# A two-layer hybrid attention kernel: store queues, buffers and loads around its stage borders, and a weave that starts with matrix work alone

## The chip, the cores and the metric

The kernel runs on one core of one Trainium2 chip. The metric is the device time of one execution in microseconds (us), the median of the runs shown. The time before is 3861.09 us, the median of three runs between 3860.72 and 3863.76.

The engines of the core appear under the profile's names: PE is the tensor engine (PEld its weight loads, which run beside the matmuls), DVE the vector engine, ACT the scalar engine, POOL the general-purpose engine and SP the engine that here only issues DMAs. ACT and POOL can issue DMAs too. Each engine takes its instructions in order, DMA issues included.

## The reference

The model has two layers over 2048 latent tokens of width 1024, with 256 context tokens ahead of them, everything in FP32. Cut to what matters:

```
h  = rms_norm(x)  * (1 + scale) + shift          # adaLN; the same for the context, hc
# layer 0 (even): latent attention A and gated linear attention B side by side
q_lat, kv_lat, k_rope, za, gq, gk, gv, g_lr, zb = split(h @ w_in)      # and for hc
q, k, v = mla_heads(q_lat, kv_lat, k_rope)       # 8 heads, 96 wide (64 + 32 rope), values 64
a = softmax(q k^T * scale) v                     # over latent and context keys
b = gla_bidirectional(gq, gk, gv, g_lr)          # scans in both directions, chunks of 64
x = x + gate * (concat(a * silu(za), rms_norm(b) * silu(zb)) @ w_out)  # context too
# layer 1 (odd): neighbourhood attention, 16 heads of 64
q, k, v, z = split(h @ w_in)
o = softmax over an 8 x 16 window of the 32 x 64 grid, with a position bias rpb, and all context keys
x = x + gate * ((o * silu(z)) @ w_out)
```

## The kernel before

The tokens are 18 row tiles (NT) of 128, of which the first two (NCT) are the context; T is all 2304 of them. Every FP32 product of activations with weights is made of three matmuls: each operand is split into a high and a low part (names that end in h or l), and `mm3` adds high x high (L114), high x low (L115) and low x high (L116); `mm3_steps` is the same as a generator, three matmuls to a step (L123 to L125). Attention scores are made of three matmuls in the same way (L889 to L892). Results that a later stage reads in another layout go to DRAM and come back: QT, KT and Vn (queries, keys and values of layer 0, high and low parts), zaT, Un (the other projections of layer 0), Q1, K1, V1, V1c, z1, M1 (those of layer 1), and RT (what the output projection reads).

The softmax has no running maximum. A stage ahead of the attention makes every score once with the high parts alone, reduces it to the maximum of each query row, and stores minus that maximum as one more row of the queries: row A_QK of QT in layer 0, M1 in layer 1. The attention's first matmul (K = 97 or 65 rows) takes it in, so the exponential follows at once.

The stages in order, with their rough place in the profiled span:

- 0 to 573, `even_latent`: for each row tile the first gemm, then `up` (query and key projections, norms, rope) and `fin`: PE transposes into `tp` (L492), the split into `qkhl` (two buffers, ACT and DVE), and four stores to QT and KT from SP (L498). `first(t, j)` makes three of the later projections of the last two tiles ahead, into one buffer `vn`, stored to Un from ACT (L512).
- 573 to 1124, `even_rest`: the remaining projections of layer 0 (`cell`, 86 cells of 8 steps, 688 steps) and the maxima (`maxes`: 8 heads, 83 steps each, 664 in all), matmul L591 and DVE reduction L592, on keys `mk` and queries `mq` loaded from KT and QT (L580, L586). Each head ends with L595 and L597 and the store of its row from ACT (L600).
- 1124 to 2067, `even_mix`: attention (`even_attention`) with the linear attention (`gla`) placed into it. The attention works through 4 pairs of heads, each over 5 query blocks (the context's 256 and four of 512). Keys `akh`, `akl` and queries `aqh`, `aql` have a tile and a load of their own for each head. `gla` loads its rows of Un as `gu` and transposes them (L640, L641).
- 2067 to 2303, `project` of layer 0, with `prep` (norm and transposes L296, L299) of the first two tiles of layer 1 and the first weight loads of it (`od_steps`, buffers `wraw`) running ahead inside.
- 2303 to 2715, `odd_qk`, and 2715 to 3191, `odd_vz`: projections of layer 1. `odd_vz` has 66 cells (528 steps); values go through `ovz` (three buffers) to V1 and V1c (`store_v`), and the maxima of 16 heads (256 steps) are woven in. Each head loads a bias table `mtab`, to which POOL adds masks (L1134, L1135), and stores its maxima to M1 in four pieces.
- 3195 to 3674, `odd_attention`, over 8 pairs of heads: queries q, context keys kc, key blocks kb, values ov, bias tables tab, score matmuls L1244 and L1245. Then `project` of layer 1, to the end.

What sets the order: the Python code emits instructions with their dependences, and a planner that simulates the engines decides the final order on each engine. `weave(main, side, ratio, lag)` steps two generators together, `ratio` steps of the side for one of the main, and bounds how far the main one may be placed ahead: its instructions are issued after the side's step that lies `lag` back. `ahead` holds generators of later weight loads that are stepped in between (`pump`).

## Time and profile before

| | before |
|---|---|
| median of 3 runs | 3861.09 us (3860.72 to 3863.76) |
| the profiled execution | 3867.9 us, its span 3866.1 us |
| PE busy | 3670.2 us, 95% of the span |
| DVE busy | 2347.1 us, 61% |
| ACT busy | 1475.4 us |
| POOL busy | 1269.1 us |
| DMA | 503.09 MB, mean 130 GB/s |

The page's rows give, for each line and engine, what an instruction writes and reads, its shape and number, its busy time and mean ns, and the idle time of its engine just before it with what ended it. A row of the waits gives engine, tile and line that waited, the engine or DMA and the tile that released it, then the total us, the number of waits and the longest. PE's clock (PEclk) is the share of its full rate that it was granted.

### The profile page before, as it was taken

To read this page: it belongs to the slowest core of one execution; us is meant where nothing else is said; L and a number is where in the kernel's file an instruction comes from. 1 tells how busy PE (TensorE), PEld (TensorE's weight loads), DVE (VectorE), ACT (ScalarE), POOL (GpSimd) and SP (SyncE) were. 2 spreads that over 40 slices of the span, in tenths; PEclk is the share of its full clock that TensorE was granted. 3 is DMA by queue.
4 is the path that set the end of the run, shared out by engine and by line. 5 is a ranking of instruction groups with operands and counts; after the bars stand their busy time and mean duration, and the time that the engine had idled before them with its cause. 6 is when DMAs were issued, how large, how long until landed. Compare 5 with 4: busy or idle time off the path is not lost. (4 is left out here: it accounts for less than half of the span.)

```text
span 3866.1 us, 52721 instructions
## 1 busy us (share of the span) xinstructions
PE 3670.2 (95%) x18388; PEld 2767.7 (72%) x18388; DVE 2347.1 (61%) x4699; ACT 1475.4 (38%) x2928; POOL 1269.1 (33%) x1356
## 2 busy tenths in 40 slices
PE   7999979999979999999999999999999997889899
PEld 4999878888866666555556788888788874555577
DVE  4677757888855556586654344444677765667632
ACT  3555541111115555545553123333322225656610
POOL 0334320000004444454543223333222215667622
PEclk8999989999989999999999999999999998999999
DMA  6455553222241232323514544445544468797553
GB/s 236 138 152 148 155 166 90 75 85 77 69 130 59 75 99 75 90 86 111 148 57 136 164 142 126 131 128 154 176 135 132 138 136 207 182 204 183 146 150 114
DMA packets 387175, 503.09 MB, mean 130 GB/s; under 512 B 30691, under 2 KB 265611, under 8 KB 380424
## 3 DMA queue, kind: packets, MB, share of 16 engines
q1 hardware_dynamic: 339174, 447.83, 41.1%
q10 hardware_dynamic: 47576, 51.37, 4.2%
q8 instruction: 146, 2.39, 0.3%
q14 instruction: 119, 0.97, 0.1%
q0 software_dynamic: 160, 0.52, 0.0%
HBM read 329.68 MB, written 169.93 MB: 129 GB/s over the span
## 5 line engine op out<-in xcount | busy, mean ns | idle before, releaser
L106 ACT ACTIVATE apt<-st 128x512 f32<-128x512 f32 (+1 forms) x592 | 346.1, 592 | 340.7 <-PE st L892 306.3
L592 DVE TENSOR_REDUCE mm<-mx 128x1 f32<-128x512 f32 (+1 forms) x656 | 393.2, 628 | 102.8 <-PE mx L591 95.5
L880 DVE TENSOR_TENSOR acc<-acc,apt 128x512 f32<-128x512 f32 x288 | 253.9, 903 | 174.9 <-ACT apt L106 173.4
L865 PE MATMUL av<-apt,av 128*64 128x512 f32 (+1 forms) x1184 | 306.9, 605 | 0.0
L880 POOL TENSOR_TENSOR acc<-acc,apt 128x512 f32<-128x512 f32 x160 | 216.4, 1366 | 238.6 <-ACT apt L106 237.9
L1291 POOL TENSOR_TENSOR oacc<-oacc,opt 128x341 f32<-128x341 f32 (+6 forms) x336 | 237.4, 738 | 116.5 <-ACT opt L106 92.9
L889 PE MATMUL st<-aqh,akh 97*128 97x512 f32 (+1 forms) x592 | 264.0, 446 | 11.1 <-ACT apt L106 5.8
L591 PE MATMUL mx<-mk,mq 96*128 96x512 f32 (+1 forms) x656 | 239.7, 375 | 9.4 <-DMA mq<-QT 8.5
L1162 DVE CUSTOM_DVE_ANT_1 mx<-mx,mtab 128x225 f32<-128x225 f32 (+13 forms) x576 | 180.8, 341 | 103.5 <-PE mx L1156 56.3
L890 PE MATMUL st<-aql,akh 96*128 96x512 f32 (+1 forms) x592 | 236.0, 399 | 1.2 <-DMA aql<-QT 1.2
L892 PE MATMUL st<-aqh,akl 96*128 96x512 f32 (+1 forms) x592 | 234.7, 397 | 0.0
L889 PEld LDWEIGHTS st<-aqh,akh 97*128 97x128 f32 x592 | 112.7, 191 | 137.9 <-issue 76.5
L106 ACT ACTIVATE u<-gm 128x352 f32<-128x352 f32 (+1 forms) x140 | 69.0, 498 | 357.8 <-PE gm L125 283.8
L1351 DVE TENSOR_TENSOR opt<-st,tab 128x64 f32<-128x64 f32 (+10 forms) x576 | 145.1, 313 | 73.1 <-PE st L1245 51.3
L570 POOL DMA_DIRECT2D Un<-u x2 | 1.4, 676 | 565.6 <-DVE u L559 565.6
L998 POOL TENSOR_TENSOR px<-py,px 128x512 f32<-128x512 f32 x68 | 91.2, 1343 | 283.9 <-DVE py L997 277.2
L865 PEld LDWEIGHTS av<-apt,av 128*64 128x64 f32 x1184 | 76.9, 137 | 143.3 <-issue 139.9
L997 DVE TENSOR_TENSOR py<-pj,gate 128x512 f32<-128x512 f32 x68 | 46.9, 690 | 218.0 <-PE pj L116 217.9
L1134 POOL TENSOR_TENSOR mtab<-mtab,maskq 128x1798 f32<-128x1798 f32 x16 | 51.4, 3212 | 325.0 <-DMA mtab<-rpb_q 251.1
L106 ACT ACTIVATE opt<-opt 128x465 f32<-128x465 f32 (+7 forms) x256 | 122.6, 497 | 53.6 <-DVE opt L1351 47.2
L1244 PE MATMUL st<-q,kt 128*128 128x480 f32 (+5 forms) x256 | 101.0, 406 | 39.1 <-ACT opt L106 20.9
L591 PEld LDWEIGHTS mx<-mk,mq 96*128 96x128 f32 x656 | 122.1, 189 | 22.2 <-issue 8.8
(419 smaller groups left out, 10301.7 us busy)
## 6 DMA issues: line engine op xcount, KB each, us to landing
q<-Q SPq DMA_DIRECT2D x48, 512.0 KB
kb<-K SPq DMA_DIRECT2D x192, 128.0 KB
H<-x ACTq DMA_DIRECT2D x36, 512.0 KB
pr<-RT SPq DMA_DIRECT2D x34, 512.0 KB
adaw<-ada_w SPq DMA_DIRECT2D x64, 256.0 KB
x<-H SPq DMA_DIRECT2D x32, 512.0 KB
wraw<-w_od SPq DMA_DIRECT2D x64, 256.0 KB
mtab<-rpb_q SPq DMA_DIRECT2D x16, 899.0 KB
```

The costliest lines, as they stand in the source:

```text
L106: return self.nc.scalar.activation(out, in_, func, **kw)
L591: mm = nc.tensor.matmul(ps[:, :w], q[:A_QK, (t % 6) * P : (t % 6) * P + P], k[:A_QK, k0 : k0 + w], start=True, stop=True)
L592: nc.vector.tensor_reduce(out=m[:, t, n : n + 1], in_=ps[:, :w], axis=AX.X, op=ALU.max)
L865: nc.tensor.matmul(av[i * 64 : i * 64 + 64, :w], V[:, kt, i * 64 : i * 64 + 64], pts[i][:, :w], start=n == 0, stop=n == len(kts) - 1)
L880: eng.tensor_tensor(out=acc[i][e][:, :w], in0=a[:, :w], in1=pts[i][:, :w], op=ALU.add)
L889: nc.tensor.matmul(ps[:, :w], kh[: A_QK + 1, ks], qh[: A_QK + 1, :w], start=True, stop=False)
L890: nc.tensor.matmul(ps[:, :w], kh[:A_QK, ks], ql[:A_QK, :w], start=False, stop=False)
L892: mm = nc.tensor.matmul(ps[:, :w], kl[:A_QK, kq : kq + P], qh[:A_QK, :w], start=False, stop=True)
L1162: nc.vector.tensor_tensor_reduce(out=s, in0=s, in1=tb[:, ri : ri + rn, ci : ci + cn], scale=1.0, scalar=-3e38, op0=ALU.add, op1=ALU.max, a ...
L1244: nc.tensor.matmul(ps, k1, q1, start=True, stop=False)
L1291: eng.tensor_tensor(out=a, in0=a, in1=pts[i][:, a0 - r0 : a1 - r0, :], op=ALU.add)
L1351: nc.vector.tensor_tensor(out=pt[:, d[0], d[1]], in0=ps[:, d[0], d[1]], in1=tabs[i][:, ri : ri + rn, ci : ci + cn], op=ALU.add)
```

## The change

1. **`weave`** gets `head`: so many main steps run before the first side step. After the side has ended, the anchor of the lag moves on with the main steps. `even_rest` weaves with ratio 1.08 and head 40 in place of 1.0, `odd_vz` with 0.57 in place of 0.5.
2. **`even_latent`**: the last two row tiles store Vn, QT and KT from POOL, and the second half of each result takes a buffer of the tag u in place of qkhl. `first` takes a buffer for each of its three j (lth, ltl, vn) and stores Un from POOL.
3. **Weave stores on POOL**: zaT, Un and the maxima's rows in `even_rest`, V1, V1c and M1 in `odd_vz`.
4. **`even_attention`** loads both heads of a pair, and the high and low parts of the queries, with one DMA each into merged tiles. For the first pair keys and values are cut at 3 and 9 key tiles, and the queries of block 1 are loaded behind the first cut. The next pair's keys are loaded at block 2, its values at block 4.
5. **Project and after**: a third `wraw` buffer for layer 1's weights, one more step between the two preps, and in `odd_attention` the first pair's values are loaded after its tables.

```diff
-    def weave(self, main, side, ratio, lag):
-        due, done = 0.0, []
+    def weave(self, main, side, ratio, lag, head=0):
+        due, done, over = -float(head * ratio), [], 0.0
         while True:
             with ExitStack() as es:
-                if len(done) > lag:
-                    es.enter_context(self.tc.issue_after(done[-lag - 1].ins))
+                n = len(done) - lag - 1 + int(over)
+                if n >= 0:
+                    es.enter_context(self.tc.issue_after(done[min(n, len(done) - 1)].ins))
...
                 r = next(side, None)
-                if r is not None:
+                if r is None:
+                    over += 1
+                else:
                     done.append(r)
...
-        sp, bufs, width = stage or (self.prp, 2, cols)
+        sp, bufs, width = stage or (self.prp, self.wbufs, cols)
...
-                nc.sync.dma_start(self.Vn[:, t, :], ...)
+                (nc.gpsimd if t >= NT - 2 else nc.sync).dma_start(self.Vn[:, t, :], ...)
...
-                        hl = self.tl(sp, [P, 4, 2, P], "qkhl", F32R, bufs=2)
+                        if t >= NT - 2 and h2:
+                            hl = self.tl(sp, [P, LAT_COLS], "u", F32R, bufs=2)[:, :1024].rearrange("p (j s t) -> p j s t", j=4, s=2)
+                        else:
+                            hl = self.tl(sp, [P, 4, 2, P], "qkhl", F32R, bufs=2)
...
-                        nc.sync.dma_start(
+                        (nc.gpsimd if t >= NT - 2 else nc.sync).dma_start(
                             dst[h2 * 4 : h2 * 4 + 4, :, :A_QK, t * P : t * P + P].rearrange("h s d t -> d (h s) t"),
...
-                u = self.tl(sp, [P, LAT_CHUNK], "vn", bufs=1)
+                u = self.tl(sp, [P, LAT_CHUNK], ("lth", "ltl", "vn")[j - 2], bufs=1)
                 self.act(u[:], ps[:])
-                nc.scalar.dma_start(self.Un[t, ...], u[:])
+                nc.gpsimd.dma_start(self.Un[t, ...], u[:])
...
-                    nc.scalar.dma_start(self.zaT[...], z[:])
+                    nc.gpsimd.dma_start(self.zaT[...], z[:])
                 elif j == 1:
-                    (nc.gpsimd if t < 2 else nc.sync).dma_start(self.Un[t, :, 1056:], u[:])
+                    nc.gpsimd.dma_start(self.Un[t, :, 1056:], u[:])
                 else:
-                    nc.scalar.dma_start(self.Un[t, :, (j - 2) * 352 : (j - 1) * 352], u[:, :352])
+                    nc.gpsimd.dma_start(self.Un[t, :, (j - 2) * 352 : (j - 1) * 352], u[:, :352])
...
-                    nc.scalar.dma_start(self.QT[h, 0, A_QK]..., r[:NT].bitcast(F32))
+                    nc.gpsimd.dma_start(self.QT[h, 0, A_QK]..., r[:NT].bitcast(F32))
...
-            self.weave(gemms, maxes(), 1.0, 30)
+            self.weave(gemms, maxes(), 1.08, 30, 40)
...
-            kh = self.tl(ap, [P, T], f"akh{i}", F32R, bufs=2)
-            cuts = (0, half, T) if j == 0 else (0, T)
+            kh = self.tl(ap, [P, 2, T], "akh", F32R, bufs=2)
+            cuts = firsts + (T,) if j == 0 else (0, T)      # firsts = (0, 3 * P, half)
...
+            q = self.tl(ap, [P, 4, 512], "aq", F32R, bufs=2)
+            nc.sync.dma_start(q[:A_QK, :, :w].bitcast(F32), self.QT[2 * j : 2 * j + 2, :, :A_QK, q0 : q0 + w]...)
...
+                early[0], _ = queries(0, 0, CTX)
+                gens = [keys(0), low(0, 0), values(0)]
+                K, L0, V = [next(g) for g in gens]
+                early[1], _ = queries(0, CTX, 512)
+                for g in gens:
+                    next(g)
+                next(gens[0])
+                L = [L0, next(low(0, 1))]
+                next(gens[2])
...
-                if j < 3 and nb > 1:
+                if j < 3 and nb in (2, 4):
                     with self.tc.issue_after(last.ins):
-                        if nb < 4:
-                            nextK[nb - 2], = keys(j + 1, nb - 2)
+                        if nb == 2:
+                            nextK, = keys(j + 1)
...
-            self.prep_pool(e1, "prp1", "left", 2)
+            self.prep_pool(e1, "prp1", "left", 2, 3)
...
                 for t in range(2):
                     hT[t] = self.prep(1, t, self.x1, pp, ("pj", 4))
+                    yield
                     yield
...
-            self.nc.scalar.dma_start(self.V1c[:, t, c], v[:])
+            self.nc.gpsimd.dma_start(self.V1c[:, t, c], v[:])
...
-            self.nc.scalar.dma_start(self.V1[a + r, g * 64 : g * 64 + 64, c], v[r * 64 : r * 64 + 64])
+            self.nc.gpsimd.dma_start(self.V1[a + r, g * 64 : g * 64 + 64, c], v[r * 64 : r * 64 + 64])
...
-                        nc.scalar.dma_start(self.M1[h, ...], ...)
+                        nc.gpsimd.dma_start(self.M1[h, ...], ...)
...
-            self.weave(gemms, maxes(), 0.5, 15)
+            self.weave(gemms, maxes(), 0.57, 15)
...
                 kc = keys(j, 0, CTX, "kc")
-                V = values(j)
...
+                else:
+                    V = values(j)
...
                 tabs = [table(2 * j + i, i) for i in range(2)]
+                if j == 0:
+                    V = values(j)
```

More of the change, by code (lines that the diff above doesn't have):

```diff
@@ L278, in ada_row, with prep_pool @@
             nc.sync.dma_start(self.gates[l, :, (b - 4) * 512 : (b - 4) * 512 + 512], row[:])
-    def prep_pool(self, es, name, side, bufs):
+    def prep_pool(self, es, name, side, bufs, wbufs):
         self.prp = self.pool(es, name, bufs=2, side=side, reuse_waits="tile")
-        self.hbufs = bufs
+        self.hbufs, self.wbufs = bufs, wbufs
     def prep(self, l, t, src, pp, tag):
@@ L808, in low @@
         def low(j, p):
-            kl = [self.tl(ap, [P, half], f"akl{p}{i}", F32R, bufs=1) for i in range(2)]
-            for i in range(2):
-                nc.sync.dma_start(kl[i][:A_QK].bitcast(F32), self.KT[2 * j + i, 1, :A_QK, p * half : (p + 1) * half])
-            return kl
-        def queries(j, q0, w):
-            Q = []
-            for i, h in enumerate((2 * j, 2 * j + 1)):
-                qh = self.tl(ap, [P, 512], f"aqh{i}", F32R, bufs=2)
-                ql = self.tl(ap, [P, 512], f"aql{i}", F32R, bufs=2)
-                nc.sync.dma_start(qh[:A_QK, :w].bitcast(F32), self.QT[h, 0, :A_QK, q0 : q0 + w])
-                nc.sync.dma_start(qh[A_QK : A_QK + 1, :w].bitcast(F32), self.QT[h, 0, A_QK : A_QK + 1, q0 : q0 + w])
-                last = nc.sync.dma_start(ql[:A_QK, :w].bitcast(F32), self.QT[h, 1, :A_QK, q0 : q0 + w])
-                Q.append((qh, ql))
-            return Q, last
@@ L826, in even_attention @@
+        nextK = nextV = None
+        early = {}
         for j in range(4):
-            rest = []
             if j == 0:
-                Q, _ = queries(0, 0, CTX)
-                gens = [keys(0, i) for i in range(2)] + [values(0)]
-                K = [next(g) for g in gens[:2]]
-                L = [low(0, 0)]
-                V = next(gens[2])
-                rest = gens
-            else:
-                K = list(nextK)
-                V = nextV
-                L = [low(j, 0), low(j, 1)]
+                early[0], _ = queries(0, 0, CTX)
[7 more added lines that the diff above has]
+                next(gens[2])
+            else:
+                K, V = nextK, nextV
+                L = [next(low(j, p)) for p in range(2)]
@@ L839, in even_attention @@
             for nb, (q0, w, kts) in enumerate(blocks):
-                if j or nb:
+                if j == 0 and nb in early:
+                    Q = early.pop(nb)
+                else:
                     Q, last = queries(j, q0, w)
@@ L850, in even_attention @@
                 yield
-                if rest:
-                    for g in rest[:2]:
-                        next(g)
-                    L.append(low(0, 1))
-                    next(rest[2])
-                    rest = []
                 av = self.tl(pp, [P, 512], "av", bufs=2)
@@ L1256, in odd_attention @@
                         pass
+                else:
+                    V = values(j)
                 if mk is None:
```

48 lines of the change are left out of this document (27 added, 21 removed).

## The prediction, made before the changed kernel was run

> **What bounds the kernel now.** I read the page's first part, then the waits of the tensor engine over the whole run, then windows cut around the largest of them, then the timelines of the DMA queues there. The page first.
>
> ```profile
> span 3866.1 us, 52721 instructions
> PE 3670.2 (95%) x18388; PEld 2767.7 (72%) x18388; DVE 2347.1 (61%) x4699; ACT 1475.4 (38%) x2928; POOL 1269.1 (33%) x1356
> L592 DVE TENSOR_REDUCE mm<-mx 128x1 f32<-128x512 f32 (+1 forms) x656 | 393.2, 628 | 102.8 <-PE mx L591 95.5
> ```
>
> PE is busy 95% of the span. The change adds and removes no matrix work, so all it can win is PE's idle time, 3866.1 - 3670.2 = 196 us, and what the idle stretches cost in clock afterwards. Where the idle time sits is in the waits: engine, line and what it waited for, then us in total, times, longest.
>
> ```profile
> engine line waited for: us in total, times, longest us
> PE st L1244 <- DMA q<-Q: 12.5, 2, 8.1
> PE gl L641 <- POOL gu L640: 10.3, 1, 10.3
> PE mx L591 <- DMA mq<-QT: 8.5, 1, 8.5
> PE gm L123 <- ACT onat L106: 7.0, 1, 7.0
> PE gm L114 <- ACT vn L106: 6.4, 1, 6.4
> PE tp L438 <- DVE qkhl L496: 5.6, 4, 3.9
> PE st L889 <- DMA aqh<-QT: 5.2, 1, 5.2
> PE pj L299 <- DVE x L296: 4.9, 1, 4.9
> PE mx L597 <- DVE mc L595: 4.4, 2, 2.5
> PE mx L1149 <- ACT mz L106: 3.7, 1, 3.7
> PE tp L492 <- DVE qkhl L496: 3.0, 3, 1.2
> PE mx L1169 <- DVE mc L1167: 2.7, 1, 2.7
> PE st L890 <- DMA aql<-QT: 1.2, 1, 1.2
> PE st L1245 <- DMA kc<-K: 1.2, 1, 1.2
> ```
>
> These are single events at borders between stages, and the windows around them show two costs: PE's busy time short of the window's length, and a granted clock (PEclk) well under 1 for the work that is done there. The columns are PE, PEld, DVE, ACT and POOL busy, PEclk, DMA share, GB/s.
>
> ```profile
> 545.00:558.00 13.00, 6.45 (x24) 6.20 (x25) 8.80 (x18) 4.58 (x7) 4.88 (x4) 0.61 0.91 272
> 573.00:586.00 13.00, 4.47 (x15) 3.93 (x15) 4.19 (x7) 1.01 (x3) 0.00 (x0) 0.61 0.97 244
> ...
> 1121.00:1132.00 11.00, 7.25 (x27) 4.94 (x27) 3.95 (x10) 2.39 (x7) 0.44 (x3) 0.53 1.08 273
> 1132.00:1156.00 24.00, 8.18 (x19) 5.55 (x20) 2.18 (x5) 3.55 (x7) 1.48 (x4) 0.57 0.72 199
> 2183.00:2194.00 11.00, 6.13 (x22) 4.90 (x21) 5.81 (x7) 5.00 (x11) 1.98 (x3) 0.69 0.47 153
> 2714.00:2726.00 12.00, 5.03 (x15) 3.67 (x14) 4.38 (x8) 4.65 (x8) 0.00 (x0) 0.72 0.80 231
> 3182.00:3222.00 40.00, 18.29 (x50) 9.92 (x49) 15.86 (x49) 8.53 (x17) 9.11 (x4) 0.57 1.00 212
> ...
> 600.00:1050.00 450.00, 449.70 (x2330) 398.25 (x2329) 366.25 (x610) 60.37 (x106) 0.00 (x0) 1.00 0.26 78
> ```
>
> So inside the weave (600 to 1050) PE never stops and runs at full clock; at the borders it loses both. I price the clock as busy time in the window times one minus PEclk, since work done at PEclk c would have taken c of that time. The last row also gives a measure for cover: 450 / 2330 = 0.19 us for one matmul of the weave.
>
> **Border 1, latent into even_rest (545 to 586).** The change gives the three Un chunks of `first` a tile each, so the 6.4 us wait on the one vn buffer has no cause left. The last two tiles' result stores go out on POOL, half of their results lie in other buffers, and the weave runs 40 gemm steps before its first max. In the changed program's order 48 matmuls of W2/WU gemms then stand between the last transposes and the first mx, and further gemms split the last kn transposes. What they must hide:
>
> ```profile
> 570.01 1.47 SPq L498 DMA_DIRECT2D KT<-qkhl  x2
> 573.38 0.32 SPq L580 DMA_DIRECT2D mk<-KT  x1
> ```
>
> The load of mk follows the issue of the last KT store, which ends at 570.01 + 1.47 = 571.48, by 1.9 us, and PE waited 8.5 us for mk and mq. 48 x 0.19 = 9.1 us of gemms hide that. The added cost is POOL: its only stores before are these two.
>
> ```profile
> L570 POOL DMA_DIRECT2D Un<-u x2: 556/676/797, 1112.6 to 1120.5; - x2
> ...
> DMA to landing us min/median/max: 2.6/5.3/7.9
> ```
>
> A landing after 2.6 to 7.9 us in place of those 1.9 makes mk later by 0.7 to 6.0; I take 2 of exposure. Ten stores of 0.7 us occupy a POOL that the rows at 573 and 600 show idle. Sum: idle 6.4 + 8.5 + 1.0 (one of the L492 waits) = 15.9; clock (6.45 + 4.47) x 0.39 = 4.3; less 2: **18 us**, bounds 10 and 20. The 3.9 us wait of L438 at 525 stays. If the 48 gemms were not ready (they need W2's weights, loaded long before), the 8.5 us would come back whole.
>
> [...]
>
> **Border 2, even_rest into even_mix (1121 to 1156).** SP and ACT show why the queries came late.
>
> ```profile
> 1124.93 0.30 ACTq L600 DMA_DIRECT2D QT<-mr  x1
> ...
> 1131.56 0.30 SPq L819 DMA_DIRECT2D aqh<-QT  x1
> 1136.69 1.24 SPq L636 DMA_DIRECT2D gu<-Un x2
> ```
>
> The last row of maxes is stored at 1124.93, the next query load is issued 6.6 us later, and the gla's gu load another 5.1 us behind it in SP's order; L889, L890 and L641 pay 5.2 + 1.2 + 10.3. With ratio 1.08 the last max ends before the last gemms (688 gemm steps and 664 max steps; 40 + 664 / 1.08 = 655), the loads are merged (SP has 1368 instead of 1490 instructions over the run), the first key pieces are cut to three key tiles, and block 1's queries go out ahead of the remaining keys. In the changed order the attention's first loads wait only for gemms some 70 to 200 matmuls ahead of its first score, and the first gl transpose stands 71 matmuls = 13.5 us behind it, while gu is issued near the start. Idle 0.7 (a wait of the last mx) + 2.5 + 5.2 + 10.3 + 1.2 = 19.9; clock 7.25 x 0.47 + 8.18 x 0.43 = 6.9; together 26.8. The DMA share of 1.08 and 0.72 says that bytes, not only order, hold the loads; I leave 4 us of wait and 2 of clock: **21 us**, bounds 10 and 27. The stores of zaT, Un and the mr rows on POOL (18 + 68 + some 8 for each max stage) meet a POOL that was busy 0.00 in the weave; ACT loses their issues, where it was busy 60 of 450 us. Both are off the path: nothing.
>
> Faster maxes load DVE: 366.25 / 450 = 81% rises by 1.08 to 88%. That is mostly the reduce of 628 ns for each mx. PE waited on it 0.7 us in all; for the denser weave, and the odd one, I charge 1 us in 100 over the 450: **-5**, bounds 0 and -12.
>
> **The smaller borders.** An extra `yield` between the two preps puts 48 matmuls (9.1 us) ahead of the second one's transposes; the 4.9 us wait for x goes, and 6.13 x 0.31 = 1.9 of clock: **6**, bounds 0 and 7. At 2714 PE waits 7.0 us for onat from ACT, which stands in order behind copies of weights that wait for loads into two wraw buffers; the third buffer lets the loads start one earlier. 7.0 + 5.03 x 0.28 = 8.4 at most; whether one buffer is enough the trace cannot show: **5**, bounds 0 and 8. The gla scan's waits keep their order: nothing, 5 either way.
>
> **Border 3, odd_vz into odd_attention (3182 to 3222).** Idle 40 - 18.29 = 21.7, clock 18.29 x 0.43 = 7.9. With 0.57 the 256 max steps are done after 449 of 528 gemm steps, and five whole cells of 24 matmuls, 120 x 0.19 = 23 us, follow without maxes; the waits for mz and mc (3.7 + 2.7) have work beside them. About 6.4 MB (by the code's shapes: queries, tables, V, the context's keys, the first key block) must land before scores run freely; at the row's 212 GB/s that is 30 us, so 7 stay open, with their clock, and the smaller waits (kc 1.2, and those on opt) stay. V1c's load still waits for the last V1c store, now POOL's. I take **13**, bounds 0 and 24.
>
> **Sum.** 18 + 21 - 5 + 6 + 5 + 13 = 58. The profiled execution took 1.8 us more than its span (3867.9), 6.8 us above the median; single waits are alike in any execution, so I take the sum from the median: 3861.1 - 58 = **3803 us**. All upper bounds together, with the scan's: 20 + 27 + 7 + 8 + 24 + 5 = 91, 3770; all lower ones: 10 + 10 - 12 - 5 = 3, 3858.
>
> **Rivals.** *The loads take it back.* The borders move at 199 to 273 GB/s with a DMA share near 1; if bytes hold them, an earlier issue gains only what the weave's tail lends. Then 2 keeps its gl part, 1 its vn part, 3 nothing: 10 + 12 - 5 + 6 + 0 = 23, 3838. For it: the DMA columns; against: the share is 0.26 in the weave before, where the new loads now begin.
>
> *Slower: POOL's order in odd_vz.* Now some 64 V1 and V1c stores and 64 M1 stores stand in one in-order queue with the adds on mtab.
>
> ```profile
> POOL mtab L1134 <- DMA mtab<-rpb_q: 251.1, 13, 30.8
> L1134 POOL TENSOR_TENSOR mtab<-mtab,maskq 128x1798 f32<-128x1798 f32 x16 | 51.4, 3212 | 325.0 <-DMA mtab<-rpb_q 251.1
> ```
>
> POOL sat 251.1 us at such adds, waiting for the table, 30.8 us at most and 19 on average. A V1 store queued behind such an add is held as long; ovz has three buffers, and at four or more cells of 24 x 0.19 = 4.6 us that is some 14 us of slack, so a 19 us wait costs PE 5 and a 30.8 us wait 17. It decides the sign when the 13 waits cost 5 or more each: 65 - 58 = 7 over. With 2 us of clock behind each gap it is 13 x 7 = 91, and 91 - 58 = 33: 3894. Against it: the planner knows the order and puts stores that are ready ahead of the adds.
>
> *No change.* The order by the changed program does what the diff says, so this needs new waits that sum to 50 to 66; for it speaks only that DVE is next in the weaves.
>
> [...]
>
> **How the numbers follow.** This kernel's measurement can tell 0.2%, 7.7 us, from no change. Forecast 0.68 (its own range 3775 to 3830); loads take it back 0.15; no change 0.04; POOL's order 0.13. Faster: 0.68 + 0.15 = 0.83, same 0.04, slower 0.13. Leaving out the slower case and a few in a hundred at the low end, the range is 3778 to 3850.
>
> **What would show it.** In the changed profile: no wait of gm on vn; mx on mq under 3 us; gl on gu and st on aq under 4 together; pj on x gone; gm on onat under 3; the first q wait near 7; PEclk near 1 around 550, 1140 and 2190; PE idle near 145 us. POOL's waits in odd_vz with ovz copies waiting on DMA would show the slower rival. DVE as PE's releaser by more than 12 us in the weaves, or a POOL store from which an mk load waits over 10 us, would make the forecast wrong.

## The result, and the profile after

The changed kernel takes 3834.48 us (median of four runs, 3830.0 to 3836.73) against 3860.9 us for the one before in the same comparison: a ratio of 0.9924, 95% interval 0.9911 to 0.9937. It is faster by 26 us where 58 were forecast, inside the stated range. The profiled execution took 3835.3 us, its span 3833.5. The profiled span of before was 3866.1, so the two traces differ by 32.6 us and not by 26.4: the profiled execution of before lay 6.8 us above its median, as the prediction noted, and the changed one 0.8. The account below is of the traces.

The page and the waits of PE after, in the same form as before:

```profile
span 3833.5 us, 52744 instructions
PE 3668.1 (96%) x18388; PEld 2758.2 (72%) x18388; DVE 2349.6 (61%) x4699; ACT 1474.7 (38%) x2928; POOL 1413.8 (37%) x1594
...
q0 software_dynamic: 13088, 32.52, 2.8%
```

```profile
PE st L1246 <- DMA q<-Q: 12.8, 1, 12.8
PE mx L604 <- DVE mc L602: 7.2, 7, 1.8
PE gm L123 <- ACT onat L106: 6.0, 1, 6.0
PE tp L442 <- DVE qkhl L503: 4.8, 4, 3.2
PE mx L1171 <- DVE mc L1169: 4.4, 9, 1.0
PE tp L496 <- POOL kn L484: 4.3, 1, 4.3
PE gm L114 <- ACT lth L106: 2.5, 1, 2.5
PE tp L572 <- DVE u L566: 2.0, 1, 2.0
```

Gone are the waits for mq (8.5), vn (6.4), the queries aqh and aql (5.2 + 1.2), gu (10.3), x in `pj` (4.9) and mz (3.7). New are kn behind POOL (4.3), lth (2.5) and u (2.0), and the waits for mc come at 7 of the 8 heads of maxima in `even_rest` and at 9 of the 16 in `odd_vz`. The windows, columns as before:

```profile
520.00:590.00 70.00, 56.48 (x279) 50.03 (x277) 34.48 (x59) 26.91 (x44) 22.86 (x27) 0.88 0.63 188
...
1115.00:1160.00 45.00, 42.45 (x185) 25.64 (x184) 16.79 (x25) 24.18 (x44) 16.30 (x18) 1.00 0.69 187
...
2155.00:2185.00 30.00, 30.00 (x138) 24.81 (x137) 13.04 (x17) 6.66 (x15) 7.16 (x7) 1.00 0.63 212
...
3155.00:3200.00 45.00, 30.41 (x135) 19.25 (x135) 13.85 (x39) 15.53 (x32) 17.70 (x14) 0.81 0.91 223
600.00:1050.00 450.00, 442.92 (x2292) 392.83 (x2291) 367.98 (x619) 58.81 (x103) 43.47 (x75) 1.00 0.24 75
```

The border into even_mix is nearly full and at full clock. But the weave, where PE was busy 449.70 of 450 us before, now has 442.92.

To see where time goes when stages shift, I laid the two traces beside each other at equal amounts of PE work: each matmul counts with the median distance to the next start among its kind, the sums of both kernels are equal, and at each point of the sum the times are subtracted. The table holds what each stretch gained (minus) or lost against before, in us; the first row is the forecast in the same cut, the others are this kernel and the experiments told below. The stretches in before's time: start to 521, border 1 to 627, even weave to 1107, border 2 to 1187, attention and gla to 2060, project 0 to 2270, odd_qk to 2673, the stage change at 2714 to 2760, odd weave to 3161, border 3 to 3307, the rest of PE's work, and the end behind it. Each row is one execution, up to 7 us off its kernel's median. Stretches that a kernel shares with the changed one agree within about 4, project 0 within 5 and the rest of PE's work within 7; border 2 and the attention run into each other, and the cut between them is uncertain by 2. The two kernels told last have no row.

```
                        start  b1  weave    b2  attn  proj   qk  2714  oddw    b3  rest  end
forecast                  0   -18     5   -21    0    -6     0    -5     0   -13     0    0
changed kernel          0.1  -8.9   6.9 -25.0  5.5  -5.6   0.8  -3.4   7.6 -16.0  -0.2  5.5
weave stores back       1.9 -11.4   5.3 -11.8  3.2  -5.3   0.3   0.3   6.4  -6.4   3.5  0.3
even_rest stores back   0.3  -8.1   5.3 -12.0  3.1  -5.5   0.7  -0.2   8.8 -14.9  -0.0  2.3
ratios back             2.3  -8.6  -1.8  -3.9 -1.1  -2.6   1.0  -2.9  -0.5   0.0   5.4  5.4
old attention loads     3.6  -9.0   6.9  -2.4  2.5  -7.1  -0.9  -0.5   9.1 -17.5  -0.7  5.4
merged loads alone      1.2  -0.1   1.6 -15.0 -2.4   0.2  -0.2  -0.1   0.4   0.6  -3.8  0.2
latent stores back      2.3  -8.5   6.9 -25.5  4.4  -3.9   0.4  -2.7   9.6 -15.4  -3.4  0.4
small parts back       -1.4  -5.6   5.3 -23.2  3.4  -0.4  -0.2   4.5   8.6 -13.3   1.7  5.4
V1c load on POOL        1.7 -11.2   5.3 -24.3  6.8  -7.1   0.8  -0.4   9.3 -10.6  -7.2  5.6
late transpose          1.0  -9.7  -3.2 -24.6  4.1  -4.3   0.8  -2.7   2.7 -16.9   1.0  5.4
first pair first        1.8  -8.1  -3.2 -24.8  3.4  -1.1   0.4  -3.1   4.8  -6.8   3.3  5.5
```

So the borders gave 8.9 + 25.0 + 5.6 + 3.4 + 16.0 = 58.9 us, close to the 63 forecast for them, and 25.5 were lost elsewhere: 14.5 in the two weaves where 5 were charged, 5.5 in the attention, 5.5 behind the last matmul.

### The profile page after: what moved, and what is told of

The parts are those of the page before. It is cut to its first block, busy times and chain, and to the rows that moved or that the text cites. A ratio compares the mean times of both kernels' runs of the same rounds, so it can differ in the third digit from the quotient of the medians.

```text
span 3833.5 us, 52744 instructions
## 1 busy us (share of the span) xinstructions
PE 3668.1 (96%) x18388; PEld 2758.2 (72%) x18388; DVE 2349.6 (61%) x4699; ACT 1474.7 (38%) x2928; POOL 1413.8 (37%) x1594
## 3 DMA queue, kind: packets, MB, share of 16 engines
q0 software_dynamic: 13088, 32.52, 2.8%
## 5 line engine op out<-in xcount | busy, mean ns | idle before, releaser
L1296 POOL TENSOR_TENSOR oacc<-oacc,opt 128x341 f32<-128x341 f32 (+7 forms) x336 | 239.1, 742 | 109.3 <-ACT opt L106 81.5
L890 PE MATMUL st<-aq,akh 97*128 97x512 f32 (+1 forms) x592 | 263.1, 445 | 4.0 <-ACT apt L106 3.9
L891 PE MATMUL st<-aq,akh 96*128 96x512 f32 (+1 forms) x592 | 234.7, 397 | 0.0
L893 PE MATMUL st<-aq,akl 96*128 96x512 f32 (+1 forms) x592 | 233.9, 396 | 0.0
L890 PEld LDWEIGHTS st<-aq,akh 97*128 97x128 f32 x592 | 111.9, 189 | 136.5 <-issue 90.7
L893 PEld LDWEIGHTS st<-aq,akl 96*128 96x128 f32 x592 | 113.1, 191 | 31.0 <-issue 5.7
L106 ACT ACTIVATE prh<-pr 128x1024 fp32r<-128x1024 f32 x34 | 35.7, 1056 | 252.1 <-PE pj L115 252.1
L598 PEld LDWEIGHTS mx<-mk,mq 96*128 96x128 f32 x656 | 120.8, 188 | 11.6
```

The lines of the kernel that those rows point to most:

```text
L106: return self.nc.scalar.activation(out, in_, func, **kw)
L598: mm = nc.tensor.matmul(ps[:, :w], q[:A_QK, (t % 6) * P : (t % 6) * P + P], k[:A_QK, k0 : k0 + w], start=True, stop=True)
L890: nc.tensor.matmul(ps[:, :w], K[: A_QK + 1, i, ks], qh[: A_QK + 1, :w], start=True, stop=False)
L891: nc.tensor.matmul(ps[:, :w], K[:A_QK, i, ks], ql[:A_QK, :w], start=False, stop=False)
L893: mm = nc.tensor.matmul(ps[:, :w], kl[:A_QK, i, kq : kq + P], qh[:A_QK, :w], start=False, stop=True)
L1296: eng.tensor_tensor(out=a, in0=a, in1=pts[i][:, a0 - r0 : a1 - r0, :], op=ALU.add)
```

## The experiments

Twelve kernels ran, each timed beside the kernel before.

| kernel | median us | before beside it | ratio, 95% interval |
|---|---|---|---|
| weave stores back | 3847.77 | 3864.92 | 0.9956 (0.9940 to 0.9971) |
| ratios back | 3856.52 | 3864.92 | 0.9973 (0.9962 to 0.9984) |
| old attention loads | 3861.85 | 3864.92 | 0.9992 (0.9982 to 1.0001) |
| latent stores back | 3835.28 | 3864.92 | 0.9925 (0.9909 to 0.9940) |
| small parts back | 3854.62 | 3862.94 | 0.9978 (0.9968 to 0.9988) |
| merged loads alone | 3851.24 | 3862.94 | 0.9963 (0.9948 to 0.9978) |
| late transpose | 3823.43 | 3862.94 | 0.9897 (0.9880 to 0.9914) |
| V1c load on POOL | 3840.39 | 3862.94 | 0.9936 (0.9922 to 0.9951) |
| first pair first | 3838.09 | 3868.51 | 0.9928 (0.9913 to 0.9942) |
| first pair, latent stores back | 3825.14 | 3868.51 | 0.9897 (0.9882 to 0.9911) |
| first pair, kn on DVE | 3831.68 | 3868.51 | 0.9907 (0.9889 to 0.9924) |
| even_rest stores back | 3848.05 | 3868.51 | 0.9954 (0.9939 to 0.9969) |

The kernel before ran slower beside these runs than in the first comparison, so the ratios are compared and not the medians; the expected times were written against 3861. The changed kernel itself was not timed again beside them: its 0.9924 is from the first comparison.

### Weave stores back

```diff
-                    nc.gpsimd.dma_start(self.zaT[...], z[:])
+                    nc.scalar.dma_start(self.zaT[...], z[:])
...
-                    nc.gpsimd.dma_start(self.Un[t, :, (j - 2) * 352 : ...], u[:, :352])
+                    nc.scalar.dma_start(self.Un[t, :, (j - 2) * 352 : ...], u[:, :352])
...
-                    nc.gpsimd.dma_start(self.QT[h, 0, A_QK]...)
+                    nc.scalar.dma_start(self.QT[h, 0, A_QK]...)
...
-            self.nc.gpsimd.dma_start(self.V1c[:, t, c], v[:])          # V1 and M1 in the same way
+            self.nc.scalar.dma_start(self.V1c[:, t, c], v[:])
```

> The changed kernel with the weaves' stores (zaT, Un and the maxima's rows in even_rest; V1, V1c and M1 in odd_vz) back on ACT and SP; the latent stores stay on POOL. In the changed kernel POOL's DRAIN at the very end lasts 9.48 us (1.55 before) and holds the end of the program by some 5.5 us. Theory A (the queue of the weave stores does not matter inside the weaves; the drain grows with the number of DMAs that POOL has issued): the last DRAIN falls to about 2 us, the waits of the maxima's transposes on mc stay (7.2 and 4.4 us), 3829. Theory B (POOL's stores are what freed ACT and SP at the borders): the waits at the borders return, 5 to 15 us in sum, 3840 to 3850. Theory C (POOL's stores hold back DVE in the weaves, and that is why mc is late): the mc waits fall to 4.4 and 3 as before, 3820.

Theory B held: 0.32% of the time, some 12 us, is lost against the changed kernel; by the table 13 us at border 2 and 10 at border 3, less 5 at the end, but this trace lies 6.5 us above its median. C fell: the waits for mc stay. A was right on the last DRAIN alone, 2.71 us here. At border 2 the wait of PE and the queues of ACT and SP behind it read as follows:

```profile
PE st L890 <- ACT apt L106: 13.2, 2, 11.9
```

```profile
1121.91 7.21 SPq L851 DMA_DIRECT2D azt<-zaT  x1
1129.22 0.26 SPq L620 DMA_DIRECT2D ge<-gate_w  x1
```

```profile
1129.70 1.29 ACT L106 ACTIVATE apt<-st 128x512 f32<-128x512 f32 x2 [2.17 <-PE st L893]
1145.24 0.63 ACT L106 ACTIVATE gw<-ge 97x512 fp32r<-97x512 f32 x1 [14.25 <-DMA ge<-gate_w]
1145.78 1.55 ACT L106 ACTIVATE apt<-st 128x512 f32<-128x512 f32 x3
```

PE waits for an st buffer that ACT's exponential frees; ACT stands 14.25 us at the copy of gla's gate weights, because that load went out at 1129.22, behind a load of zaT that held SP for 7.21 us. In the changed kernel the same loads and the same copy are these:

```profile
1118.88 0.34 SPq L851 DMA_DIRECT2D azt<-zaT  x1
1119.33 0.26 SPq L620 DMA_DIRECT2D ge<-gate_w  x1
```

```profile
1135.30 0.63 ACT L106 ACTIVATE gw<-ge 97x512 fp32r<-97x512 f32 x1 [2.01 <-DMA ge<-gate_w]
```

In both kernels the copy starts 16 us after the load was issued; with the stores back the load was issued 10 us later, and PE waited for it through ACT. So the stores act at the border, through the order of SP and then of ACT. Why the load of zaT held SP for 7.21 us, the trace does not say.

### even_rest stores back

Only the stores of even_rest were put back, in the same way.

> The changed kernel with only even_rest's stores (zaT, Un, the maxima's rows) back on ACT and SP; odd_vz's and the latent ones stay on POOL. With all weave stores back the border into even_mix lost 13 us and that into odd_attention some 10 against the changed kernel. Theory A (each border depends on its own stage's stores): the first of the two comes back, the second border stays as in the changed kernel, 3846. Theory B (the stores of odd_vz made all of it): 3835. The last DRAIN, with 154 DMAs from POOL: by their number it would last some 7 us, by the latent stores alone 9.

Theory A: border 2 falls to 12.0, border 3 keeps 14.9. PE's wait for apt is there again, 11.8 us at its longest. Each border depends on its own stage's stores. The last DRAIN took 6.30 us, with 148 DMAs from POOL and not the 154 expected.

### Ratios back

```diff
-            self.weave(gemms, maxes(), 1.08, 30, 40)
+            self.weave(gemms, maxes(), 1.0, 30, 40)
...
-            self.weave(gemms, maxes(), 0.57, 15)
+            self.weave(gemms, maxes(), 0.5, 15)
```

> The changed kernel with the ratios 1.0 (head 40 kept) and 0.5 in the two weaves. Theory A (the denser weave is what makes PE wait for mc, 5.4 us more in even_rest and 6.5 in odd_vz): the weaves win some 9 + 8 us, but the maxima end with or behind the gemms and the borders into even_mix and odd_attention lose 10 to 25 us: 3828 to 3845, and the mc waits in the weaves under 1 us each. Theory B (the borders' gain comes from the order of the loads, not from the weave ending early): borders stay as they are, 3818. Theory C (POOL's stores make the mc waits): the waits stay and the borders lose, 3850.

Theory A, more strongly than expected. The weaves win back 8.7 and 8.1 us, and the borders lose 21 and 16: border 3's whole gain, and all but 4 us of border 2. B and C fell. The end of even_rest shows what an uncovered tail of maxima is:

```profile
1080.00:1100.00 20.00, 20.00 (x94) 16.42 (x93) 14.96 (x25) 2.40 (x4) 2.08 (x3) 1.00 0.64 152
1100.00:1120.00 20.00, 18.74 (x44) 10.23 (x43) 19.40 (x37) 1.88 (x2) 0.56 (x1) 0.67 1.00 261
1120.00:1140.00 20.00, 17.67 (x46) 9.45 (x46) 9.31 (x18) 4.17 (x10) 1.61 (x6) 0.50 0.44 120
```

```profile
1106.40 19.14 PE L598 MATMUL mx<-mk,mq 96*128 96x512 f32 x35 [0.21 <-DVE mm L599]
```

Between 1100 and 1120 DVE is busy 19.40 of 20 us and PE starts 44 matmuls, against 94 in the 20 us before, though its busy column still says 18.74; the clock is at 0.67, then 0.50. The 35 matmuls of maxima from 1106.40 on stand 0.55 us apart, where matmuls of the weave stood 0.21 us apart (20 / 94); DVE's 37 instructions in its 19.40 us keep the same pace. This kernel keeps head 40 at ratio 1.0, so its maxima end later than those of the kernel before: the run shows the price of a late end, and not only the loss of an early one.

### Old attention loads, and merged loads alone

The first puts `even_attention`'s loads of before into the changed kernel, the second puts the new ones into the kernel before; the whole of part 4 of the change, one way and the other.

> The changed kernel with even_attention's loads as before (a tile and a load for each head, cuts at 9 key tiles only, queries of block 1 not ahead). The border into even_mix won 28.6 us against the 21 forecast. Theory A (merged, cut and early loads carry about half of it): waits of the first scores on queries of 5 to 10 us come back with half clock behind them, 3848. Theory B (the maxima that end before the last gemms carry it; loads then start early in either form): border as in the changed kernel, 3835. In both, the 7 us that the attention lost between 1160 and 1340 against before would go if they come from the merged tiles: 3841 or 3828 then.

> The kernel before with only even_attention's new loads (merged tiles, cuts at 3 and 9 key tiles, block 1's queries early); ratios, stores and buffers as before. With the old loads in the changed kernel nearly all of its gain at the border into even_mix went. Theory A (the border is a chain of three links, maxima that end early, their stores on a queue that is free, few early loads, and each alone gains little): within 5 us of before, 3857 to 3865. Theory B (the loads alone carry the border): 15 to 25 us faster, 3840 to 3850.

The first fell on the side of A and beyond it: border 2 keeps 2.4 of 25.0 us, and with the weaves' cost nothing is left of the whole change (0.9992). The waits that return are other ones than I expected, gla's and not the scores':

```profile
PE gl L648 <- POOL gu L647: 9.2, 1, 9.2
PE gl L654 <- DVE gw L624: 6.4, 1, 6.4
```

The second lies between its theories: the loads alone win 15.0 us at border 2, 0.37% in all. So the loads carry more than half of that border by themselves, while ending early and storing from POOL carry almost nothing without them (2.4). With the loads the two add 10. The attention's 5.5 us loss is 2.5 with the old loads, 4.1 with late transposes, and turns to a gain of 1 to 2 wherever the ratios are the old ones. So the merged tiles alone are not its cause; with the uncertainty of the cut, more is not shown.

### Latent stores back

```diff
-                (nc.gpsimd if t >= NT - 2 else nc.sync).dma_start(self.Vn[:, t, :], ...)   # QT, KT too
+                nc.sync.dma_start(self.Vn[:, t, :], ...)
...
-                nc.gpsimd.dma_start(self.Un[t, ...], u[:])
+                nc.scalar.dma_start(self.Un[t, ...], u[:])
```

> The changed kernel with the last two latent tiles' stores of Vn, QT and KT back on SP and those of the first rest chunks back on ACT; the extra buffers stay. In the changed kernel PE waits 4.3 us for kn, whose multiplication stands on POOL behind a store that waits for DVE. Theory A (POOL's in-order stores are that wait): it goes, but SP is blocked in four weight loads for 8.9 us around 545, so the stores go out late and the first mx waits 3 to 8 us on mq: 3832 to 3840. Theory B (SP is not late, 48 gemms hide all): 3829. Theory C (the kn wait comes from DVE's chain, not from POOL's order): the wait stays at 3 to 4 us and mq is added: 3842.

Theory B came nearest: 0.9925 against 0.9924, and border 1 at 8.5 against 8.9. The wait for kn goes and longer waits for qkhl, u and lth take its place. The stores on POOL are worth nothing at border 1; by exclusion the buffers and the 40 steps made its gain, and no run parts these two. The end is shorter by 5 us in this trace (DRAIN 4.25), which the ratios, with intervals of 6 us to each side, do not show. In the changed kernel POOL's queue shows how the kn wait came about:

```profile
557.45 0.82 POOL L505 DMA_DIRECT2D QT<-qkhl  x1 [2.48 <-DVE qkhl L503]
558.26 0.59 POOL L519 DMA_DIRECT2D Un<-ltl  x1
558.85 0.81 POOL L505 DMA_DIRECT2D QT<-u  x1
559.67 0.63 POOL L484 TENSOR_TENSOR kn<-kbase,sqk 128x256 f32<-128x256 f32 x1
```

DVE's part of kn, and PE's transposes behind both:

```profile
557.73 0.68 DVE L483 TENSOR_TENSOR kn<-kn,sqk 128x512 f32<-128x512 f32 x1
```

```profile
560.35 1.94 PE L496 MATMUL tp<-ident,kn 128*96 128x128 f32 x8 [4.27 <-POOL kn L484]
```

The next tile's multiplication stands behind a store that waits for DVE's qkhl of this one, and PE's transposes stand behind the multiplication. But DVE's own part of kn stands behind the same qkhl and was done only at 558.41; POOL's was done at 560.30. So POOL's order makes at most 1.9 of the 4.3 us.

### Small parts back

```diff
-            self.prep_pool(e1, "prp1", "left", 2, 3)
+            self.prep_pool(e1, "prp1", "left", 2, 2)
...
                     hT[t] = self.prep(1, t, self.x1, pp, ("pj", 4))
                     yield
-                    yield
```

and the first pair's values ahead of its tables.

> The changed kernel without its fifth part: two wraw buffers, one step between the two preps, the first pair's values loaded ahead of its tables. Theory A (the account of the changed kernel's trace): the wait of pj on x of 4.9 us and its half clock come back (7 us), the third wraw buffer brought nothing (onat 6.0 against 7.0 before, so within 2), the order of values and tables moves the first q wait by under 3: 3843. Theory B (the prep's cover comes from other moves): 3835, no wait on x.

It cost 0.54%, some 20 us, where theory A said 8. The wait for x came back as expected (5.2 us; project 0 loses 5.2). The third `wraw` buffer was worth far more than the nothing of theory A: 7.9 us at the stage change against the changed kernel. The other kernels with three buffers lie between -3.4 and 0.3 there, so its worth is 4 to 8. Three edits went back at once; that this stretch is the buffer's is argued from its place. The buffer hardly shortens the wait for onat (7.7 here, 6.0 to 7.8 with three buffers), but those of ACT for weights, over the run:

```profile
ACT w3h L106 <- DMA wraw<-w_od: 23.2, 13, 3.5
ACT w1h L106 <- DMA wraw<-w_od: 22.3, 13, 5.0
ACT w2h L106 <- DMA wraw<-w_od: 15.3, 10, 2.7
```

In the changed kernel the same three are:

```profile
ACT w1h L106 <- DMA wraw<-w_od: 14.2, 8, 6.0
ACT w3h L106 <- DMA wraw<-w_od: 10.1, 12, 1.9
ACT w2h L106 <- DMA wraw<-w_od: 8.1, 7, 1.9
```

With two buffers two PE waits of 2.6 us (tp on ovz) and 2.3 us (mx on mm) follow right behind the wait for onat; that the late copies on ACT push this work back is argued. The remaining us are spread over borders 1, 2 and 3 and the rest, none of them over 3.3.

### Late transpose

```diff
-                    ps = self.tl(pp, [P, 512], "mx", bufs=5)
-                    mm = nc.tensor.transpose(ps[:NT, :P], mc[:], self.ident[:])
-                    ...                                  # mr, its store, yield
+                    late = h, mc                         # made behind step 6 of the next head
...
+                            if late is not None and n0 == 6:
+                                mm = close(*late)
+                                late = None
+                                yield mm
```

In odd_vz the same behind the step of R == 3.

> The changed kernel with the transpose of each head's maxima (and the store of its row) moved behind the sixth max step of the next head in even_rest and the fourth in odd_vz. Theory A (PE's loss in the denser weaves is its wait for DVE's reduction of mc, 7.2 + 4.4 us in the groups, some 16 us over both weaves): waits on mc under 2 us in sum, both weaves back near the rate of before, 3822. Theory B (DVE is full at the new ratio, and PE will wait for a free mx buffer instead): waits of mx on mm appear, 3832.

Theory A. All waits on mc are gone from the list, which had 7.2 and 4.4 us of them, and the same window of the weave is full again, at the denser ratio:

```profile
600.00:1050.00 450.00, 450.00 (x2347) 400.18 (x2346) 375.15 (x633) 61.10 (x108) 45.22 (x78) 1.00 0.25 77
```

DVE is busy 375.15 of 450 us, and PE waited for mm only 0.3 us over the whole run, in the odd weave. So DVE was not full at ratio 1.08; PE stood behind a transpose that came in its order before DVE had reduced the last maxima of its head. The ratio, 0.9897, is better than the changed kernel's 0.9924; the intervals (0.9880 to 0.9914 and 0.9911 to 0.9937) just overlap. The odd weave keeps 2.7 us of its loss.

### V1c load on POOL, and first pair first

```diff
-                nc.sync.dma_start(V[:, :NCT, :], self.V1c[:, :, c])
+                (nc.sync if j > 1 else nc.gpsimd).dma_start(V[:, :NCT, :], self.V1c[:, :, c])
```

> The changed kernel with the loads of the context's values of the first two pairs in odd_attention issued from POOL, where their stores are, in place of SP. In the changed kernel SP stands still from 3151 to 3161.4 in front of the load ov<-V1c, and the queries behind it come 12.8 us late for PE. Theory A (that wait in SP's order is the 12.8): the first q wait falls to 4 to 7 us, 3827. Theory B (the loads of kc and q wait for the last gemm's buffers and for bandwidth anyway): the wait stays at 10 or more, 3834.

Theory B's sign came: the first q wait is 15.9 us. The wait for the V1c store that held SP for 10.4 us in the changed kernel (first row) was not, alone, what PE waited for. With it gone, the five loads of V behind it hold SP for 9.10 us (second row), and kc goes out at 3164.64, where it was 3163.93:

```profile
SPq L1234 <- DMA V1c<-ovz: 10.4, 1, 10.4
```

```profile
3154.60 9.10 SPq L1236 DMA_DIRECT2D ov<-V  x5
```

Next the second pair's loads, which SP issues ahead of the first pair's kc and q:

```diff
+                if j == 1:
+                    with self.tc.issue_after(q0last.ins):      # first pair's last query load
+                        V = values(j)
+                        tabs = [table(2 * j + i, i) for i in range(2)]
```

on top of the late transposes.

> The kernel with the late transposes, and in odd_attention the second pair's values and tables held back until the first pair's queries are issued. With the context's values moved off SP the first q wait stayed (15.9 us), so that store was not its cause. Theory A (the second pair's loads, 2 x 517 KB of tables and 8 x 128 KB of values, stand ahead of the first pair's kc and q on SP, and these are issued only at 3164 to 3170, when the last gemms are over): the first q wait falls from 11.9 to 3 to 6 us, with some clock 8 us less, 3815. Theory B (DMA bandwidth holds the border, not the order): the wait falls by under 3, 3822. Theory C (the second pair then starts late, 60 us on): 5 us or more come back there, 3820.

Theory C won: the wait fell by 3, from 11.9 to 9.0 us, and border 3 as a whole lost 10 (6.8 against 16.9). The waits for opt are longer now, by theory C because the second pair starts late:

```profile
PE st L1266 <- DVE opt L1383: 22.5, 22, 6.9
PE st L1266 <- DMA q<-Q: 9.0, 1, 9.0
```

With the late transposes alone the first of them was this:

```profile
PE st L1265 <- DVE opt L1375: 17.6, 25, 1.8
```

The planner's order was better than mine. That the bytes of both pairs set the pace here is not shown; the DMA share of 0.91 between 3155 and 3200 in the changed kernel speaks for it.

### First pair with latent stores back, and with kn on DVE

Both stand on the kernel of "first pair first"; the first adds the edit of "latent stores back", the second that of "V1c load on POOL" and `kn` of the last two tiles on DVE.

> As the run beside it (late transposes, first pair first), and the last two latent tiles' stores on SP, those of the first rest chunks on ACT. Theory A (the POOL stores of the latent border win 2 to 3 us there and cost 5.2 at the end, where POOL's DRAIN lasts 9.48 us with them and 4.25 without): 3812, 3 us under the run beside it. Theory B (the length of the DRAIN goes by something else): DRAIN stays near 9 us and the time is 2 us over the run beside it.

> As the first of these runs (late transposes, first pair first), with the kn multiplication of the last two latent tiles on DVE in place of POOL, and the context's values of the first two pairs loaded from POOL. Theory A (PE's 4.3 us wait for kn comes from POOL's in-order stores, and SP's wait at the load of V1c is next once the second pair is out of the way): the kn wait goes, the first q wait falls by 2 to 4 us against the first run, 3809. Theory B (the kn wait is DVE's chain; q waits for its buffers): both stay within 1 us, 3815.

The first gained against "first pair first" (0.9897 against 0.9928), with the DRAIN at 4.25 us as theory A said, but by 13 us where it said 3. Of the 9.8 us between the traces 5.1 are the end, and 5.5 lie in project 0, which the edit does not touch. The second gained less surely (0.9907, its interval overlaps). There theory A holds for q and not for kn:

```profile
PE tp L496 <- DVE kn L484: 2.8, 1, 2.8
...
PE st L1267 <- DMA q<-Q: 2.7, 1, 2.7
```

The kn wait is smaller but follows DVE now (it was 6.1 us beside it, 4.3 in the changed kernel), while with V1c off SP and the second pair held back the first q wait is down from 9.0 to 2.7: so the two seem to stand one behind the other, and neither edit alone shows it. Border 3 is 13.9 there, but 9.5 us are lost in the rest, where waits for POOL's oacc (6.4 us at the longest) and for DVE's rl (10.0, ahead of the last projection) appear. Late transposes alone remain as good as any of them.

## Why the prediction was right or wrong, step by step

**Where it was right.** The change wins at single stage borders, and the sum over them was close: 58.9 us against 63. That is in part luck, since border 1 gave half of its term and borders 2 and 3 more than theirs. Prep was 5.6 for 6, border 2 25.0 for 21, border 3 16.0 for 13, and its first q wait stayed, though at 12.8 and not 7. With the ratio of before border 3 wins nothing (0.0), so the early end is needed for it, as forecast. The 449 of 528 steps in the prediction would leave nearly ten cells of gemms and not the five that it took; in the trace 131 gemm matmuls, five and a half cells, stand between the last matmul of the maxima and the first score. The rival of POOL's order in odd_vz did not come: POOL's waits in that stage show the table adds last reached when their loads had landed.

```profile
POOL V L1088 <- ACT ovz L106: 125.3, 22, 22.6
POOL M L1175 <- ACT mr L106: 85.1, 14, 13.2
...
POOL mtab L1136 <- DMA mtab<-rpb_q: 25.3, 10, 4.4
```

25.3 us of waits for tables in place of 251.1: POOL now spends its time at stores that wait for ACT, and the loads land meanwhile.

**Its own signs.** The waits for vn, mq, gu, the queries of layer 0 and x in `pj` are gone or under their bounds, as it said. PE's idle time is 165.4 us and not 145, gm on onat 6.0 and not under 3, and PEclk is 0.87 between 545 and 558. DVE as PE's releaser in the weaves comes to 7.2 + 4.4 = 11.6 us for mc in the lists, just under the 12 that it had named as too much.

**Border 1, the term mis-sized by half** (8.9 for 18). The waits for mq and vn went as said. The step that failed is counting them as won in full, with nothing behind them. PE is idle 22.1 us of the 106 from 521 to 627 before, and still 13.3 of the 97 from 521 to 618 in the changed kernel, where the waits for kn (4.3), lth (2.5) and u (2.0) are new. This idle time alone gives 8.8 of the 8.9 us: the 4.3 put down for the clock are not seen in the time, though PEclk rises from 0.87 to 0.91. "Ten stores occupy a POOL that is idle" was wrong as a reading, since POOL carries kn and the norms of the last tile too, but it is not the 9 us that are missing: with the stores back on SP and ACT the wait for kn goes, the waits for qkhl ahead of the transposes (2.7 in place of 1.0), u (3.7) and lth (3.1) are longer, and border 1 stays at 8.5.

**The weaves, a term and a zero** (14.5 for 5). I charged both weaves 1 us in 100 for DVE, but worked it out on the 450 us of the even one alone, so the odd one got nothing. The price was at another place: the wait of each head's transpose for mc, 7.2 and 4.4 us in the lists. Moving the transpose wins 10.1 us in the even weave and 4.9 in the odd one. I had read the single wait of L597 at the end (2.5) as an end effect; it was the first sign that DVE's last reductions lag the order.

**The stage change at 2714** (3.4 for 5): the size was near, the mechanism wrong. The wait for onat stayed at 6.0; ACT's waits for the weights behind it are shorter with the third buffer, and the run without it puts its worth at 4 to 8 us.

**Attention, 5.5 for nothing.** Not explained. It goes with the new ratios; the merged tiles alone do not bring it.

**The end, 5.5 for nothing.** It was put at nothing because no row of before showed a cost: POOL's DRAIN there lasts 1.55 us and here 9.48. More on it below.

**Border 2, right in sum, wrong in parts.** I gave the early end, the stores and the loads as one list of edits that add up. They form a chain: the loads alone give 15.0, stores and early end without the loads 2.4, loads and early end without the stores 12.0, loads and stores without the early end 3.9. The last two are less than the loads alone give: the early end adds only where the stores have moved too, and head 40 at ratio 1.0 makes the maxima end later, with DVE alone. The stores of `even_rest`, which the prediction put at nothing because POOL and ACT were idle enough, thus carry 13 us here; they act through the order in which SP and ACT come to the next stage's loads. And the early end is smaller than reckoned: 18 gemm matmuls follow the last maximum in the trace, where 655 of 688 steps would leave 99.

**POOL's stores** lasted about the 0.7 us that the prediction took for each of them, so border 1 did not fall short by longer ones. All in the changed kernel lasted 0.5 to 0.9 us, at that border and in weaves where DVE was busy 82% (368 of 450 us) and 75% (324 of 430) of the time:

```profile
L505 POOL DMA_DIRECT2D QT<-qkhl x2: 817/846/876, 542.6 to 557.4; - x2
...
L1088 POOL DMA_DIRECT2D V<-ovz x60: 521/548/583, 2704.0 to 3128.9; - x60
```

336 of DVE's 368 us in `even_rest` were reductions of matmul results; how long such stores last beside other work of DVE was not measured.

## What to carry to other kernels

Where a side stream that another engine bounds is woven into matrix work, let the side end before the main stream does, and place whatever closes a piece of the side (here a transpose of reduced maxima) some steps into the next piece: in this kernel the first is worth 37 us at the borders for 17 in the weaves, with loads and stores moved too, and the second takes 15 of the 17 back. A store moved to an idle engine's queue must be read against what else that engine has in order at that place (here at most 1.9 of the 4.3 us that PE waited for kn), and edits at one border that each remove a link of the same chain are not added: run them alone and left out. When loads are re-ordered by hand at a border where the DMA engines are nearly full (share 0.91 here), what is let ahead can be paid by what comes next (the first q wait fell by 3 us, the border lost 10).

## What the runs showed of the hardware that was not expected

**POOL's DRAIN at the end is long after many DMAs from POOL.** It is an instruction of POOL's sequencer at the end of the program; the longest in the changed kernel, in the trace of its line, took 9.48 us:

```profile
L1480 POOLq DRAIN  x3: 40/102/9482, 3823.2 to 3833.2; - x3
```

The program's last store was issued from SP at 3824.53 and SP's own DRAIN stands at 3827.5; the end waited for POOL until 3832.7. The length over the kernels, by DMAs issued from POOL: 1.55 us for 2, 2.71 for 16, 6.30 for 148, 9.48 for 240, 9.64 for 242, and the same to 0.01 us in every kernel with the same number. But it is 4.25 for 226, where the 14 latent stores alone are missing from the 240. Number or packets (160, 1472, 6912, 13088, 13184, and 11776) alone do not give it; what does, stays open.

**The clock falls without a long wait.** In the tail of maxima with the ratios back, PE's only listed waits were 2.3 and 0.9 us, yet PEclk went to 0.67 and 0.50 while PE started half as many matmuls as before in the same time (44 and 94). PE's busy column does not show it; its count does. By that run's rows the matmuls from 1106.40 on stood 0.55 us apart, and DVE, busy 19.40 of the 20 us up to 1120 at the same pace, is read as what spaced them. What makes the granted clock fall in such a stretch, no run shows.
